# A two-layer trunk on one core: blocks 0 and 1 of the last output product as a pair of seven products

## The chip, the cores and the metric

The kernel runs on one core of one Trainium2 chip. Its engines are TensorE (PE, with the weight loads shown as PEld), VectorE (DVE), ScalarE (ACT), GpSimd (POOL) and SyncE (SP, which here only issues transfers). The metric is the device time of one execution in microseconds; lower is better. Three runs of the kernel before took 1144.73, 1144.99 and 1146.62 us.

## The reference

A residual stream of 256 tokens by 2048 (fp32) goes through two layers, each behind an RMSNorm, and through a last RMSNorm.

```python
def gmlp_branch(xn, w_in, v_g, w_s, b_s, w_out):          # layer 0
    proj = xn @ w_in                                       # [u | v | gate], 3 x 4096
    ...
    y = u * mixed * jax.nn.silu(zg)
    return y @ w_out

def stick_breaking_branch(xn, w_in, w_out):                # layer 1
    proj = xn @ w_in                                       # [q | k | v | gate], 4 x 2048
    q, k, v, zg = jnp.split(proj, 4, axis=-1)
    ...
    o = o.reshape(B, S, SB_WIDTH) * jax.nn.silu(zg)
    return o @ w_out                                       # 2048 x 2048

def reference(x, norm_g, a_w_in, a_v_norm_g, a_w_s, a_b_s, a_w_out, b_w_in, b_w_out, final_g):
    h = x
    for i in range(DEPTH):
        hn = rms_norm(h, norm_g[i])
        ...
        h = h + y
    return rms_norm(h, final_g)
```

The edit is in the last product, `o @ w_out` of layer 1, whose 2048 output columns are four blocks of 512 (blocks 0 to 3).

## The kernel before

**Three terms.** Each fp32 operand is split into a high and a low part (`cut`: ScalarE casts the high part, line 114; VectorE subtracts it, line 115). A product of two tiles is three matmuls, high by high, high by low, low by high (`terms`, lines 119 to 121). Tokens are the stationary side (two tiles of 128, t = 0 and 1), weights the moving side (128 x 512).

**A pair.** `Pair` computes two neighbouring column blocks at once. Of the 16 k tiles of the contraction it takes `ks` tiles from each half (4, or 5 with a "fifth" tile), and does this 2 x 2 block product (two token tiles, two halves of k, two columns) with seven products instead of eight, in the Winograd form. The parts of the weights are named by half and column (`b11`, `b12`, `b21`, `b22`; in tile names b00, b01, b10, b11, then a number for two k tiles). Products p1, p2 and p4 take y itself; p5, p6, p7 and p3 take four sums of y, made once per layer by `sums_of` (tile `ys`) and `fifth` (tile `yse`). The weight sums are made by VectorE in place (lines 286 and 314) and by adding transfers that POOL issues (line 294). `head()` issues p1 and p5, `body()` p6, p2, p7, p3 and p4. Five PSUM banks a, b, c, d, e hold the results; banks a and d are column 0, b and c column 1.

The k tiles left over are plain: `column(0)` adds them to the first column at the end of `body`, and `column(1)` is kept as `pending`, whose steps the next pair takes between its own products (`run`). A raw tile for plain k tiles comes from three buffers (`wraw`), a split tile from five (`wspl`).

**The gates.** The last two pairs of `b_w_in` (bg0, bg2) make the gates. When a column is done, `evac_g` applies SiLU (tiles `bsg` in the buffers sg0 and sg1), and two entries of `queue`, `turn`, transpose it (`gT`), multiply it into `yf`, and split the result into `y_hi` and `y_lo`. Entries of `queue` run between products (`tick`).

**The last product, before.** After bg2 the plain tiles of its second column are flushed. Blocks 0 (f0) and 1 (f1) are `product`s: eight double k tiles, two token tiles, three terms. Beside f0 (`beside_f0`) the queue is drained, the residual h is read back (tile h2), and the sums of y are made at its 10th k tile. f1's steps lie between those of the head of the last pair, f2 (blocks 2 and 3, `KS_F` = 5). `finish` adds the residual, and takes squares and gains. f2's column 1 is done one token tile after the other, so that the first can be stored early (`store`).

**Order.** The program is written in this order, and a scheduler places the instructions of each engine by its own estimate of time. From the middle of bg2 on, `chain` keeps SP's loads in the written order; SP's queue is first in, first out, so a load that waits for its buffer holds back all behind it.

Of the kernel before, what the change touches and what calls it, by code (L numbers as in the profile page):

```python
# [8 lines left out]
F32 = mybir.dt.float32  # L9
F32R = mybir.dt.float32r  # L10
# [4 lines left out]
P = 128  # L15
EPS = 1e-6
NEVER = -1e30
CB = 512
# [11 lines left out]
def trunk_kernel(ctx: ExitStack, tc: tile.TileContext, x, xt, gcols, wst, a_w_in, a_v_norm_g,  # L30
# [11 lines left out]
    nc = tc.nc  # L42
    PSUM = bass.MemoryType.PSUM
    NT, D = x.shape[1], x.shape[2]
# [4 lines left out]
    H = D // P  # L49
# [12 lines left out]
    jk = ctx.enter_context(tc.tile_pool(name="jk", bufs=2))  # L62
# [25 lines left out]
    def f(ap):  # L88
        return ap.bitcast(F32)
# [16 lines left out]
    low = [None]  # L106

    def cut(raw, n, name, by=2):

        hi = wspl.tile([P, 2, CB], F32R, tag="hi", name=f"{name}_hi")  # L110
        lo = wspl.tile([P, 2, CB], F32R, tag="lo", name=f"{name}_lo")
        for i in range(0, n, by):
            sl = slice(i, min(i + by, n))
            nc.scalar.copy(hi[:, sl], raw[:, sl])  # L114
            low[0] = nc.vector.tensor_sub(lo[:, sl], raw[:, sl], f(hi[:, sl]))  # L115
        return hi, lo

    def terms(acc, lh, ll, hi, lo, first, last):
        nc.tensor.matmul(acc, lh, hi, start=first, stop=False, skip_group_check=True)  # L119
        nc.tensor.matmul(acc, lh, lo, start=False, stop=False, skip_group_check=True)  # L120
        nc.tensor.matmul(acc, ll, hi, start=False, stop=last, skip_group_check=True)  # L121
# [78 lines left out]
    queue, wait = [], [0]  # L200

    def tick(n):

        wait[0] -= n
        if wait[0] <= 0 and queue:
            wait[0], work = queue.pop(0)
            work()

    def drain():
        while queue:  # L210
            queue.pop(0)[1]()
# [4 lines left out]
    def ins_of(x):  # L216
        return x.ins if hasattr(x, "ins") else x
# [3 lines left out]
    def load(out, in_, behind=False):  # L221

        ins = ins_of(nc.sync.dma_start(out, in_))
        if behind and not chain:

            tc.add_manual_dep(ins, before[0], NOSYNC, reason="order of loads")
        before[0] = ins.name
        if chain:
            if chain[0] is not None:
                tc.add_manual_dep(ins, chain[0], NOSYNC, reason="order of loads")  # L230
            chain[0] = ins.name
# [139 lines left out]
    adds, pending, prior, ex = [], [], [], None  # L371

    def run(pair):

        tail = pending.pop() if pending else iter(())

        steps = (3 if len(pair.groups) > 2 else 2) * len(pair.groups)
        n, i = prior.pop() if prior else 0, 0

        def between():  # L380
            nonlocal i
            for _ in range((i + 1) * n // steps - i * n // steps if i < steps else 0):
                next(tail, None)
            i += 1
            if i == steps:
                flush(tail)
        for _ in pair.head():
            between()
        pair.body(between)
        pending.append(pair.column(1))  # L390
        prior.append(len(pair.rest) // 2)

    def flush(tail=None):
        for _ in tail if tail is not None else (pending.pop() if pending else ()):
            pass

    def product(src, left, ks, name, evac, before=None):

        banks = [ps_acc.tile([P, CB], F32, tag="acc", name=f"{name}_acc{t}") for t in range(NT)]
        for k0 in ks[::2]:
            if before is not None:
                before(k0)
            raw = wraw.tile([P, 2, CB], F32, tag="raw", name=f"{name}_{k0}_raw")
            load(raw, src(k0, 2))
            hi, lo = cut(raw, 2, f"{name}_{k0}")
            for kk in range(2):
                for t in range(NT):
                    lh, ll = left.part(k0 + kk, t)  # L410
                    terms(banks[t], lh, ll, hi[:, kk, :], lo[:, kk, :], k0 + kk == ks[0], k0 + kk == ks[-1])
            if k0 == ks[-2]:
                for t in range(NT):
                    evac(t, banks[t])
            tick(2)
            yield

    def columns(w, c0, c1):

        w3 = w.rearrange("(k p) n -> p k n", p=P)  # L420

        def src(k0, n, j):
            n0 = (c0, c1)[j]
            return w3[:, k0:k0 + n, n0:n0 + CB]
        return src

    def block_of(w, n0, n):
        w3 = w.rearrange("(k p) n -> p k n", p=P)
        return lambda k0, m: w3[:, k0:k0 + m, n0:n0 + n]
# [7 lines left out]
    def home(tag, shape, dtype, name):  # L437
        return big.tile(shape, dtype, tag=tag, name=name)
# [148 lines left out]
    with ExitStack() as lg:  # L587
# [35 lines left out]
        def evac_gu(b, j, t, bank):  # L623
            y = v_of(t, b * CB, CB)
            sg = jk.tile([P, CB], F32, tag=f"sg{t}", bufs=1, name=f"{'gu'[j]}{b}_{t}")
            nc.scalar.activation(sg, bank, (AF.Silu, AF.Gelu_apprx_tanh)[j], scale=r1[:, t:t + 1])
            if j == 0:
                nc.vector.tensor_mul(y, y, sg)
            else:

                queue.append((1, lambda: times(y, sg)))
# [14 lines left out]
        for b in range(NV):  # L646
            run(Pair(columns(a_w_in, 2 * W + b * CB, b * CB), left, KD, f"gu{b}", KS_GU[b],
                     lambda j, t, bank, b=b: evac_gu(b, j, t, bank), mid=lambda pair, b=b: mid_gu(b, pair), fifth_first=True))
# [147 lines left out]
    p = o_pair(0, None, evac_pair0)  # L796
# [11 lines left out]
    p = o_pair(2, evac_o, mid_o2)  # L808
    p.body(beside(p, g, 1))
    tail = p.column(1)  # L810
    while len(queue) > TPB // 2:
        queue.pop(0)[1]()
    p = Pair(columns(b_w_in, 0, D), left1, KD, "qk0", 4, lambda j, t, bank: evac_qk(0, j, t, bank),
             mid=lambda pair: drain())
# [12 lines left out]
    yf = home("x_hi", [P, H, S], F32, "yf")  # L827
# [171 lines left out]
    pe = y_hi = y_lo = None  # L999
# [9 lines left out]
    def evac_g(hg, t, bank):  # L1009
        sg = gates[t] = jk.tile([P, CB], F32, tag=f"sg{t}", bufs=1, name=f"bsg{hg}_{t}")  # L1010
        nc.scalar.activation(sg, bank, AF.Silu, scale=r2[:, t:t + 1])
        if t == 0:
            return
        sgs = dict(gates)

        def turn(k2):
            pt = ps_ms.tile([P, 2, S], F32, tag="ms", name=f"gT{hg}_{k2}")
            transposed(pt, lambda j, t: sgs[t][:, (k2 * 2 + j) * P:(k2 * 2 + j + 1) * P])
            e0 = hg * TPB + k2 * 2
            sl = slice(e0, e0 + 2)  # L1020
            nc.vector.tensor_mul(yf[:, sl, :], pt, yf[:, sl, :])
            nc.scalar.copy(y_hi[:, sl, :], yf[:, sl, :])
            nc.vector.tensor_sub(y_lo[:, sl, :], yf[:, sl, :], f(y_hi[:, sl, :]))
        for k2 in range(TPB // 2):
            queue.append((1, lambda k2=k2: turn(k2)))

    p.body()
    pending.append(p.column(1))
    prior.append(len(p.rest) // 2)
# [5 lines left out]
    yl = Left(None, None)  # L1035
# [4 lines left out]
    for hg in (0, 2):  # L1040
        run(Pair(columns(b_w_in, 3 * D + hg * CB, 3 * D + (hg + 1) * CB), left1, KD, f"bg{hg}", KS_B,
                 lambda j, t, bank, hg=hg: evac_g(hg + j, t, bank), mid=in_order if hg == 2 else None))
    flush()


    h = gf = None
# [5 lines left out]
    def finish(c, t, acc):  # L1052
        nc.vector.tensor_add(part_of(t, c), acc, part_of(t, c))
        if c == 1:
            later.append((c, t))
        else:
            square_f(c, t, part_of(t, c))
            gain_f(c, t)
# [7 lines left out]
        junk = pe.tile([P, CB], BF16, tag="junk", bufs=2, name=f"junkf{c}_{t}")  # L1066
        nc.scalar.activation(junk, hb, AF.Square, accum_out=sqf[:, t, c:c + 1])

    def beside_f0(k0):

        nonlocal h, gf
        if k0 == 0:
            yl.hi, yl.lo = y_hi, y_lo
        elif k0 == 8:
            drain()
            h = home("v0", [P, NT, D], F32, "h2")
            load_h2(0)
            gf = pe.tile([P, D], F32, name="gf")
            with tc.issue_after(ins_of(low[0])):
                nc.gpsimd.dma_start(gf, final_g.rearrange("(o d) -> o d", o=1).to_broadcast([P, D]))  # L1080
        elif k0 == 10:

            yl.sums_of((yf[:, 0:4], yf[:, 4:8]), 4, home("xs", [P, 2, 4, 4, P], F32R, "ys"), "ys_sm")
            yl.fifth(jk.tile([P, 2, 4, 1, P], F32R, tag="more", bufs=1, name="yse"), "yse")

    def load_h2(c):
        load(h[:, :, c * CB:(c + 1) * CB], hs[:, :, c * CB:(c + 1) * CB])
# [36 lines left out]
    def residual(pair, t):  # L1124
# [2 lines left out]

    last = []

    flush(product(block_of(b_w_out, 0, CB), yl, list(range(H)), "f0", lambda t, bank: finish(0, t, bank), beside_f0))  # L1130
    f1 = product(block_of(b_w_out, CB, CB), yl, list(range(H)), "f1", lambda t, bank: finish(1, t, bank),
                 lambda k0: load_h2(1 + k0 // 4) if k0 in (0, 4, 8) else None)
    p = Pair(columns(b_w_out, 2 * CB, 3 * CB), yl, H, "f2", KS_F,
             lambda j, t, bank: finish(2, t, bank), mid=mid_f)
    for _ in range(2):
        next(f1)
    for _ in p.head():
        next(f1)
    flush(f1)
    p.body()  # L1140


    last = [cut(raw, 2, f"fl_{i}") for i, raw in enumerate(last)]
# [48 lines left out]
```

## Time and profile before

| | |
|---|---|
| runs | 1144.73, 1144.99, 1146.62 us (median 1144.99) |
| profiled execution, first to last instruction (span) | 1142.0 us; the page gives no other time for it |
| median of the runs less the span | 3.0 us |
| TensorE busy | 1132.3 us, 99% of the span |
| VectorE busy | 1010.9 us, 89% |
| ScalarE busy | 828.5 us, 73% |
| HBM read | 259.55 MB, 231 GB/s over the span with what is written |
| mean granted TensorE clock | 0.999 |

"Busy" counts the time in which an instruction runs. TensorE's matmuls are pipelined: each is shown as 0.39 us long, and the next one starts before it ends. The chain of work that ended last is followed back from the last instruction; the share of an engine in it says how much of the span that engine set. Row names leave out buffer numbers: f_p_lo is the low part of a tile of some product p of the pairs f0 and f2, f_lo that of a plain tile.

### The profile page before, as it was taken

Reading aid. Unit: us, or ns where it says so; the run is one execution under the profiler, and the core shown is the slowest. Engines: PE = TensorE matmul, PEld = TensorE weight load, DVE = VectorE, ACT = ScalarE, POOL = GpSimd, SP = SyncE. Lnnn points to the kernel's source line nnn. Section 1 sums busy time; section 2 is a strip of 40 time slices with the busy share of each in tenths; the row PEclk is TensorE's granted clock in tenths of the full one; section 3 lists DMA queues with packets and bytes.
Section 4 is the critical chain, followed back from the end, with each engine's and each line's share of the span. In section 5 each row is a group of like instructions: output and inputs, shape, how many; then the busy total and the mean of one; then the engine's idle time right before and its main releaser. Section 6 shows DMA issues by size and latency. Waiting matters only on the chain.

```text
span 1142.0 us, 14838 instructions
## 1 busy us (share of the span) xinstructions
PE 1132.3 (99%) x5168; PEld 937.6 (82%) x5168; DVE 1010.9 (89%) x1111; ACT 828.5 (73%) x1102; POOL 99.8 (9%) x106
## 2 busy tenths in 40 slices
PE   9999999999999999999999999999999999999997
PEld 6788888888888888888888888888888888888886
DVE  7899889988998999978988678989889989897996
ACT  8776777777777778866657456788678887886564
POOL 0100110110110210100010001110100101100000
PEclk9999999999999999999999999999999999999999
DMA  9988788787797797685885868687687776837972
GB/s 335 317 290 270 214 252 270 194 266 241 173 274 249 191 261 240 177 296 142 267 259 166 276 203 282 153 280 211 181 283 200 211 230 174 272 88 241 325 225 92
DMA packets 135659, 264.72 MB, mean 232 GB/s; under 512 B 8992, under 2 KB 9504, under 8 KB 135456
## 3 DMA queue, kind: packets, MB, share of 16 engines
q1 hardware_dynamic: 117472, 227.57, 58.9%
q0 software_dynamic: 16304, 33.04, 16.2%
q10 hardware_dynamic: 1808, 3.17, 0.8%
q8 instruction: 40, 0.66, 0.2%
q14 instruction: 35, 0.29, 0.1%
HBM read 259.55 MB, written 4.19 MB: 231 GB/s over the span
## 4 chain that ended last, share of the span: by engine, by line
PE 93%; DMA 2%; DVE 2%; issue 1%; ACT 1%; SPq 0%; POOLq 0%; POOL 0%; ACTq 0%; DVEq 0%
PE gu_a L119 3%; PE gu_b L119 3%; PE gu_b L121 3%; PE gu_a L121 3%; PE gu_a L120 3%; PE gu_b L120 3%; PE op_acc L119 2%; PE op_acc L120 2%; PE op_acc L121 2%; PE gu_d L119 2%; PE gu_d L121 2%; PE gu_c L121 2%; PE gu_d L120 2%; PE gu_c L119 2%; PE gu_c L120 2%; PE qk_a L121 1%
## 5 line engine op out<-in xcount | busy, mean ns | idle before, releaser
L114 ACT CAST gu_p_hi<-gu_b 128x1024 fp32r<-128x1024 f32 (+1 forms) x126 | 122.9, 1004 | 38.4 <-DVE gu_b L314 16.1
L115 DVE TENSOR_TENSOR gu_p_lo<-gu_b,gu_p_hi 128x1024 fp32r<-128x1024 f32 (+1 forms) x126 | 142.8, 1165 | 1.9 <-ACT gu_p_hi L114 1.2
L115 DVE TENSOR_TENSOR qk_p_lo<-qk_b,qk_p_hi 128x1024 fp32r<-128x1024 f32 (+1 forms) x77 | 80.8, 1073 | 8.9 <-ACT qk_p_hi L114 8.4
L114 ACT CAST qk_p_hi<-qk_b 128x1024 fp32r<-128x1024 f32 (+1 forms) x77 | 70.5, 934 | 19.0 <-DMA qk_b<-in_b_w_in 4.0
L115 DVE TENSOR_TENSOR gu_lo<-gu_raw,gu_hi 128x1024 fp32r<-128x1024 f32 x60 | 72.1, 1218 | 12.5 <-ACT gu_hi L114 12.2
L114 ACT CAST gu_hi<-gu_raw 128x1024 fp32r<-128x1024 f32 x60 | 62.0, 1052 | 21.0 <-DMA gu_raw<-in_a_w_in 11.5
L115 DVE TENSOR_TENSOR v_lo<-v_raw,v_hi 128x1024 fp32r<-128x1024 f32 (+1 forms) x41 | 48.9, 1193 | 15.2 <-ACT v_hi L114 15.2
L114 ACT CAST v_hi<-v_raw 128x1024 fp32r<-128x1024 f32 (+1 forms) x41 | 41.7, 1028 | 27.9 <-DMA v_raw<-in_a_w_in 26.4
L115 DVE TENSOR_TENSOR v_p_lo<-v_b,v_p_hi 128x1024 fp32r<-128x1024 f32 x42 | 50.3, 1220 | 3.3 <-ACT v_p_hi L114 3.1
L114 ACT CAST v_p_hi<-v_b 128x1024 fp32r<-128x1024 f32 x42 | 43.0, 1049 | 9.8 <-PE v_c L121 4.9
L115 DVE TENSOR_TENSOR bg_p_lo<-bg_b,bg_p_hi 128x1024 fp32r<-128x1024 f32 (+1 forms) x42 | 42.5, 1041 | 4.8 <-ACT bg_p_hi L114 4.7
L114 ACT CAST o_p_hi<-o_b 128x1024 fp32r<-128x1024 f32 (+1 forms) x35 | 33.4, 965 | 18.1 <-PE op_acc L121 13.0
L115 DVE TENSOR_TENSOR bv_p_lo<-bv_b,bv_p_hi 128x1024 fp32r<-128x1024 f32 (+1 forms) x42 | 42.5, 1040 | 3.8 <-ACT bv_p_hi L114 3.6
L114 ACT CAST bv_p_hi<-bv_b 128x1024 fp32r<-128x1024 f32 (+1 forms) x42 | 37.4, 908 | 10.0 <-DMA bv_b<-in_b_w_in 3.0
L294 POOL DMA_DIRECT2D gu_b<-in_a_w_in x20 | 23.0, 1155 | 240.2 <-DVE gu_b L286 134.3
L114 ACT CAST bg_p_hi<-bg_b 128x1024 fp32r<-128x1024 f32 (+1 forms) x42 | 37.3, 907 | 8.0 <-PE bg_a L121 2.5
L115 DVE TENSOR_TENSOR o_p_lo<-o_b,o_p_hi 128x1024 fp32r<-128x1024 f32 (+1 forms) x35 | 38.3, 1113 | 5.4 <-ACT o_p_hi L114 5.4
L286 DVE TENSOR_TENSOR gu_b<-gu_b,gu_b 128x1024 f32<-128x1024 f32 (+1 forms) x36 | 41.4, 1169 | 0.1
L114 ACT CAST o_hi<-o_raw 128x1024 fp32r<-128x1024 f32 x22 | 23.0, 1052 | 24.9 <-DMA o_raw<-in_a_w_out 24.8
L115 DVE TENSOR_TENSOR o_lo<-o_raw,o_hi 128x1024 fp32r<-128x1024 f32 x22 | 26.7, 1221 | 15.2 <-ACT o_hi L114 15.0
L114 ACT CAST op_hi<-op_raw 128x1024 fp32r<-128x1024 f32 x24 | 25.1, 1053 | 19.3 <-PE op_acc L121 8.8
L120 PE MATMUL op_acc<-op_lo,yc 128*128 128x512 f32 x96 | 37.8, 393 | 0.0
(798 smaller groups left out, 3797.8 us busy)
## 6 DMA issues: line engine op xcount, KB each, us to landing
gu_b<-in_a_w_in SPq DMA_DIRECT2D x64, 512.0 KB, 4.8
gu_raw<-in_a_w_in SPq DMA_DIRECT2D x60, 512.0 KB, 5.4
v_raw<-in_a_w_in SPq DMA_DIRECT2D x39, 512.0 KB, 5.5
qk_b<-in_b_w_in SPq DMA_DIRECT2D x32, 512.0 KB, 5.3
qk_raw<-in_b_w_in SPq DMA_DIRECT2D x26, 512.0 KB, 5.5
v_b<-in_a_w_in SPq DMA_DIRECT2D x24, 512.0 KB, 5.4
op_raw<-in_a_w_out SPq DMA_DIRECT2D x24, 512.0 KB, 4.9
o_raw<-in_a_w_out SPq DMA_DIRECT2D x22, 512.0 KB, 4.7
```

Of the source, the lines that this page charges most:

```text
L114: nc.scalar.copy(hi[:, sl], raw[:, sl])
L115: low[0] = nc.vector.tensor_sub(lo[:, sl], raw[:, sl], f(hi[:, sl]))
L119: nc.tensor.matmul(acc, lh, hi, start=first, stop=False, skip_group_check=True)
L120: nc.tensor.matmul(acc, lh, lo, start=False, stop=False, skip_group_check=True)
L121: nc.tensor.matmul(acc, ll, hi, start=False, stop=last, skip_group_check=True)
L286: nc.vector.tensor_sub(into[g], b0[g], b1[g])
L294: adds.append(nc.gpsimd.dma_start(into[g], self.src(HALVES[i][k], n, j), accum_op=ALU.add))
```

## The change

Blocks 0 and 1 become a `Pair` with four k tiles from each half (f0, `ks` = 4). It is run like the pairs ahead: its head and body take the steps of bg2's second column between their products, and its own second column lies between the products of f2. The turns of the second gate block are called before it (`turned` notes which are done), the sums of y are made ahead of it, and what stood beside f0 moves to its middle (`mid_f0`, called between p4 and the plain tiles of column 0).

```diff
+            turned.append(e0)
...
-    flush()
...
-        if k0 == 0:
-            yl.hi, yl.lo = y_hi, y_lo
-        elif k0 == 8:
-            drain()
...
-        elif k0 == 10:
-
-            yl.sums_of((yf[:, 0:4], yf[:, 4:8]), 4, home("xs", [P, 2, 4, 4, P], F32R, "ys"), "ys_sm")
-            yl.fifth(jk.tile([P, 2, 4, 1, P], F32R, tag="more", bufs=1, name="yse"), "yse")
+    def mid_f0(pair):
+        drain()
+        h = home("v0", [P, NT, D], F32, "h2")
+        load_h2(0)
+        load_h2(1)
...
+        yl.fifth(jk.tile([P, 2, 4, 1, P], F32R, tag="more", bufs=1, name="yse"), "yse")
...
-    flush(product(block_of(b_w_out, 0, CB), yl, list(range(H)), "f0", lambda t, bank: finish(0, t, bank), beside_f0))
-    f1 = product(block_of(b_w_out, CB, CB), yl, list(range(H)), "f1", lambda t, bank: finish(1, t, bank),
-                 lambda k0: load_h2(1 + k0 // 4) if k0 in (0, 4, 8) else None)
+    while H // 2 - 2 not in turned:
+        queue.pop(0)[1]()
+    yl.hi, yl.lo = y_hi, y_lo
+    yl.sums_of((yf[:, 0:4], yf[:, 4:8]), 4, home("xs", [P, 2, 4, 4, P], F32R, "ys"), "ys_sm")
+    run(Pair(columns(b_w_out, 0, CB), yl, H, "f0", 4, lambda j, t, bank: finish(j, t, bank), mid=mid_f0))
+    load_h2(2)
+    load_h2(3)
...
-    for _ in range(2):
-        next(f1)
-    for _ in p.head():
-        next(f1)
-    flush(f1)
-    p.body()
+    run(p)
+    pending.clear()
```

Three places of the order show it. In the names, f0_p40 is the first two k tiles of f0's product p4, f0_08 the plain double tile of k 8 and 9 in column 0, f0_18 the same in column 1, and ys the sums of y.

VectorE, where the sums of y are made. Before, this is in the second half of block 0 and the start of block 1:

```order
L1023 TENSOR_TENSOR y_lo_9017<-yf_6081,y_hi_9016 128x512
L115 TENSOR_TENSOR f0_12_lo_9581<-f0_12_raw_9578,f0_12_hi_9580 128x1024
L184 TENSOR_TENSOR ys_9532<-ys_sm_0_9533,ys_9532 128x512
L1023 TENSOR_TENSOR y_lo_9017<-yf_6081,y_hi_9016 128x512
L184 TENSOR_TENSOR ys_9532<-ys_sm_1_9534,ys_9532 128x512
L115 TENSOR_TENSOR f0_14_lo_9599<-f0_14_raw_9596,f0_14_hi_9598 128x1024
L189 TENSOR_TENSOR ys_sm_0_9533<-yf_6081 128x512
L190 TENSOR_TENSOR ys_sm_1_9534<-yf_6081,ys_sm_1_9534 128x512
L115 TENSOR_TENSOR f1_0_lo_9628<-f1_0_raw_9625,f1_0_hi_9627 128x1024
L184 TENSOR_TENSOR ys_9532<-ys_sm_0_9533,ys_9532 128x512
```

VectorE, the same sums now, between the products of f0:

```order
L286 TENSOR_TENSOR f0_b00_1_9371<-f0_b10_1_9503,f0_b00_1_9371 128x1024
L115 TENSOR_TENSOR f0_p21_lo_9552<-f0_b10_1_9503,f0_p21_hi_9551 128x1024
L115 TENSOR_TENSOR f0_p70_lo_9563<-f0_b01_0_9373,f0_p70_hi_9562 128x1024
L190 TENSOR_TENSOR ys_sm_1_9356<-yf_6081,ys_sm_1_9356 128x512
L184 TENSOR_TENSOR ys_9354<-ys_sm_0_9355,ys_9354 128x512
L115 TENSOR_TENSOR f0_p71_lo_9573<-f0_b01_1_9375,f0_p71_hi_9572 128x1024
L115 TENSOR_TENSOR f0_p30_lo_9587<-f0_b11_0_9424,f0_p30_hi_9586 128x1024
L334 TENSOR_TENSOR f0_b_9507<-f0_b_9507,f0_es_9509 128x512
L115 TENSOR_TENSOR f0_p31_lo_9597<-f0_b11_1_9426,f0_p31_hi_9596 128x1024
L115 TENSOR_TENSOR f0_p40_lo_9607<-f0_b00_0_9369,f0_p40_hi_9606 128x1024
L184 TENSOR_TENSOR ys_9354<-ys_sm_1_9356,ys_9354 128x512
```

Per plain tile two or three operations on sums stood ahead; now they lie among tiles of seven products that themselves need differences of weights, and the fourth sum stands behind p4's first tile.

VectorE, the eviction of block 0 (line 1053 before, 1054 now). Before:

```order
L286 TENSOR_TENSOR f2_b00_0_9661<-f2_b01_0_9667,f2_b00_0_9661 128x1024
L168 TENSOR_TENSOR yse_sm_9549<-yse_full_9548,yse_sm_9549 128x128
L170 TENSOR_TENSOR yse_sm_9549<-yse_full_9548,yse_sm_9549 128x128
L1053 TENSOR_TENSOR h2_9510<-f0_acc0_9428,h2_9510 128x512
L1053 TENSOR_TENSOR h2_9510<-f0_acc1_9429,h2_9510 128x512
L172 TENSOR_TENSOR yse_9547<-yse_sm_9549,yse_9547 128x512
L1063 TENSOR_TENSOR h2_9510<-h2_9510,gf_9512 128x512
L115 TENSOR_TENSOR f1_4_lo_9688<-f1_4_raw_9685,f1_4_hi_9687 128x1024
```

The same eviction on VectorE now, at the head of f2:

```order
L115 TENSOR_TENSOR f2_p12_lo_9761<-f2_b00_2_9731,f2_p12_hi_9760 128x512
L286 TENSOR_TENSOR f2_b00_0_9727<-f2_b01_0_9733,f2_b00_0_9727 128x1024
L1054 TENSOR_TENSOR h2_9627<-f0_a_9377,h2_9627 128x512
L286 TENSOR_TENSOR f2_b00_1_9729<-f2_b01_1_9735,f2_b00_1_9729 128x1024
L1054 TENSOR_TENSOR h2_9627<-f0_d_9582,h2_9627 128x512
L286 TENSOR_TENSOR f2_b00_2_9731<-f2_b01_2_9737,f2_b00_2_9731 128x512
L1064 TENSOR_TENSOR h2_9627<-h2_9627,gf_9630 128x512
L115 TENSOR_TENSOR f0_18_lo_9770<-f0_18_raw_9767,f0_18_hi_9769 128x1024
L115 TENSOR_TENSOR f2_p50_lo_9797<-f2_b00_0_9727,f2_p50_hi_9796 128x1024
```

The eviction, which reads f0's finished banks, stands between differences of f2's weights and ahead of f0_18, the first plain tile of block 1.

SP's loads around the last plain tile of block 0 (14 before, 014 now). Before:

```order
L223 DMA f0_14_raw_9596<-in_b_w_out 128x2x512
L223 DMA h2_9510<-hs_4513 128x2x512
L223 DMA f1_0_raw_9625<-in_b_w_out 128x2x512
L223 DMA f1_2_raw_9643<-in_b_w_out 128x2x512
L223 DMA f2_b00_0_9661<-in_b_w_out 128x2x512
L223 DMA f2_b00_1_9663<-in_b_w_out 128x2x512
L223 DMA f2_b00_2_9665<-in_b_w_out 128x512
```

SP's loads there now:

```order
L223 DMA f0_014_raw_9699<-in_b_w_out 128x2x512
L223 DMA h2_9627<-hs_4513 128x2x512 x2
L223 DMA f2_b00_0_9727<-in_b_w_out 128x2x512
L223 DMA f2_b00_1_9729<-in_b_w_out 128x2x512
L223 DMA f2_b00_2_9731<-in_b_w_out 128x512
L223 DMA f2_b01_0_9733<-in_b_w_out 128x2x512
L223 DMA f2_b01_1_9735<-in_b_w_out 128x2x512
L223 DMA f2_b01_2_9737<-in_b_w_out 128x512
L223 DMA f0_18_raw_9767<-in_b_w_out 128x2x512
```

The first loads of f2 follow the last plain tile of block 0 without plain tiles between them, and the first plain tile of block 1 stands behind them.

More of the change, by code (lines that the diff above doesn't have):

```diff
@@ L1023, in turn @@
             nc.vector.tensor_sub(y_lo[:, sl, :], yf[:, sl, :], f(y_hi[:, sl, :]))
+            turned.append(e0)
         for k2 in range(TPB // 2):
             queue.append((1, lambda k2=k2: turn(k2)))
+    turned = []
     p.body()
@@ L1067, in square_f @@
         nc.scalar.activation(junk, hb, AF.Square, accum_out=sqf[:, t, c:c + 1])
-    def beside_f0(k0):
+    def mid_f0(pair):
         nonlocal h, gf
-        if k0 == 0:
-            yl.hi, yl.lo = y_hi, y_lo
-        elif k0 == 8:
-            drain()
[L1076 to L1080, printed above, removed]
-        elif k0 == 10:
-            yl.sums_of((yf[:, 0:4], yf[:, 4:8]), 4, home("xs", [P, 2, 4, 4, P], F32R, "ys"), "ys_sm")
-            yl.fifth(jk.tile([P, 2, 4, 1, P], F32R, tag="more", bufs=1, name="yse"), "yse")
+        drain()
+        h = home("v0", [P, NT, D], F32, "h2")
+        load_h2(0)
+        load_h2(1)
+        gf = pe.tile([P, D], F32, name="gf")
+        with tc.issue_after(ins_of(low[0])):
+            nc.gpsimd.dma_start(gf, final_g.rearrange("(o d) -> o d", o=1).to_broadcast([P, D]))
+        yl.fifth(jk.tile([P, 2, 4, 1, P], F32R, tag="more", bufs=1, name="yse"), "yse")
     def load_h2(c):
```

## The prediction

> **What bounds the kernel now.** I read the chain that ended last, then what TensorE waits for, then the busy time by stretch around the edit, then VectorE's timeline there, since it writes the low half of each weight tile that TensorE multiplies.
>
> ```profile
> span 1142.0 us, 14838 instructions
> PE 93%; DMA 2%; DVE 2%; issue 1%; ACT 1%; SPq 0%; POOLq 0%; POOL 0%; ACTq 0%; DVEq 0%
> PE wps L79 <- DVE warm L76: 1.3, 1, 1.3
> PE v_acc L120 <- DVE v_lo L115: 0.6, 1, 0.6
> PE gT L434 <- ACT bsg L1011: 0.2, 1, 0.2
> ...
> 982.00:1026.90 44.90, 44.90 (x220) 37.86 (x219) 40.72 (x45) 38.83 (x51) 4.17 (x4) 1.00 0.53 140
> 1026.90:1060.00 33.10, 32.91 (x161) 27.13 (x160) 24.85 (x30) 22.07 (x30) 0.56 (x1) 1.00 0.73 236
> 1060.00:1102.90 42.90, 42.90 (x191) 35.53 (x190) 38.09 (x48) 23.48 (x31) 4.14 (x4) 1.00 0.91 296
> 1102.90:1126.00 23.10, 23.10 (x104) 19.04 (x103) 22.77 (x27) 16.44 (x22) 0.00 (x0) 1.00 0.36 115
> ```
>
> TensorE holds the chain, and once started it waits under 1 us in all. So a matmul removed is time gained, as long as TensorE goes on finding its operands ready. Columns of the last four rows: stretch, length, then busy time of PE, weight load, DVE, ACT, POOL, then granted clock, DMA share, GB/s. From 1026.9 to 1102.9 (the last gate pair's plain k tiles, blocks 0 and 1, the first products of the last pair) VectorE is busy 24.85 + 38.09 = 62.9 of 76.0 us: 13.1 us are free. Behind that it is full: 22.77 of 23.10.
>
> **Removed: twelve matmuls.** Blocks 0 and 1 took 2 x 16 k tiles x 2 token tiles x 3 terms = 192 products of 128x512. The pair takes 7 x 4 x 3 = 84, and 8 k tiles x 2 columns x 2 x 3 = 96: 180.
>
> ```profile
> 1130.52 0.39 PE L119 MATMUL f_c<-fl_hi,y_hi 128*128 128x512 f32 x1
> 1134.37 0.39 PE L121 MATMUL f_c<-fl_hi,y_lo 128*128 128x512 f32 x1
> 1034.27 0.65 PE gT L434 x6
> ```
>
> These are the first and last of 18 in a row: (1134.37 - 1130.52) / 17 = 0.2265 us each; a transpose is 0.65 / 6 = 0.11. Term one: 12 x 0.2265 = **-2.7 us**.
>
> **Added: VectorE work.** The pair cuts 7 x 2 + 4 + 4 = 22 double tiles where 16 were cut, and forms 6 sums or differences of double tiles: 12 more operations of 128x1024. Two sums with a bank copy make two more of 128x512. The sums of y, the turns of the gates and the evictions keep their number and only move.
>
> ```profile
> 1057.65 0.68 DVE L185 TENSOR_TENSOR ys_sm<-yf 128x512 f32<-128x512 f32 x1
> 1058.25 0.68 DVE L1021 TENSOR_TENSOR yf<-gT,yf 128x512 f32<-128x512 f32 x1
> 1068.81 0.89 DVE L165 TENSOR_TENSOR yse_full<-y_hi,y_lo 128x128 f32<-128x128 f32 x4
> 1069.62 0.28 DVE L169 TENSOR_TENSOR yse_sm<-yse_full 128x128 f32<-128x128 f32 x1
> 1116.98 3.48 DVE L115 TENSOR_TENSOR f_lo<-f_raw,f_hi 128x1024 fp32r<-128x1024 f32 x3
> 1120.38 3.48 DVE L115 TENSOR_TENSOR fl_lo<-fl_raw,fl_hi 128x1024 fp32r<-128x1024 f32 x3
> ```
>
> Back to back, start to start: 3.40 / 3 = 1.135 us for 128x1024, 0.60 for 128x512, 0.81 / 4 = 0.20 for 128x128. The addition is 12 x 1.135 + 2 x 0.60 = 14.8 us, and it must be done in 2.7 us less. The 13.1 free microseconds are short of that by 14.8 + 2.7 - 13.1 = 4.4 us, unless VectorE has a lead to spend. So I keep two accounts from a point that both kernels share.
>
> ```profile
> 1026.97 1.22 DVE L115 TENSOR_TENSOR bg_lo<-bg_raw,bg_hi 128x1024 fp32r<-128x1024 f32 x1
> 1027.98 0.40 PE L119 MATMUL bg_a<-bg_hi,x 128*128 128x512 f32 x1
> 1029.12 0.69 DVE L1023 TENSOR_TENSOR y_lo<-yf,y_hi 128x512 fp32r<-128x512 f32 x1 [0.33 <-ACT y_hi L1022]
> 1031.58 1.23 DVE L115 TENSOR_TENSOR bg_lo<-bg_raw,bg_hi 128x1024 fp32r<-128x1024 f32 x1 [1.15 <-ACT bg_hi L114]
> ```
>
> VectorE starts the low part of the last gate pair's tile 010 at 1026.97, TensorE its first product at 1027.98: there is no lead. The next two idles, 0.33 + 1.15 = 1.48 us, lie before the two orders part and stay.
>
> - To the low part of f0's product p4 (f0_p40) VectorE has 25 operations of 128x1024 and 20 of 128x512 ahead and with it: 28.4 + 12.0, so 1067.4, and 1068.9 with the 1.48. TensorE has 151 products and 18 transposes before it needs that tile: 34.2 + 2.0, so 1064.1. TensorE is then late by 4.8 us (by the same count it is 3.0 at p71, three tiles earlier).
> - The eviction of block 0 (h2<-f0_a) now stands in VectorE's order between two differences of f2's tiles. TensorE reaches the end of f0_a after 219 products and 24 transposes, at 1080.2, with the delay 1085.0, and the last product takes 0.39 more. VectorE arrives at 1084.4 and waits 1.0 us; in the kernel before the like wait was 0.5:
>
> ```profile
> 1126.18 0.69 DVE L1053 TENSOR_TENSOR h<-f_a,h 128x512 f32<-128x512 f32 x1 [0.52 <-PE f_a L121]
> ```
>
> - To the low part of block 1's first plain tile (f0_18) VectorE has 35 of 128x1024, 32 of 128x512, 8 of 128x128: 39.7 + 19.3 + 1.6 = 60.6, so 1087.6. TensorE needs it after 237 products and 24 transposes: 53.7 + 2.6, so 1084.3. The gap is 3.3; with 1.48 and 1.0 it is **+5.8 us**, term two. Later tiles up to the last (f2_014) need no more by the same accounts (f0_114 and f2_p71 come within 0.4 us of it).
>
> Term three is what VectorE idles beside that, which no row of before can show, since there it never led the time here.
>
> ```profile
> 1000.00:1010.00 10.00, 10.00 (x56) 8.65 (x55) 9.38 (x11) 8.60 (x13) 0.86 (x1) 1.00 0.40 76
> 1010.00:1020.00 10.00, 10.00 (x47) 8.35 (x46) 9.65 (x12) 8.38 (x11) 0.00 (x0) 1.00 0.36 105
> ```
>
> Low end 0: from 1096.56 to 1126.18 it runs without a gap. High end: in these windows it idles 0.97 of 20 us, 5%, over the 56 us from 1034 to 1090 that is 2.7. Nearest is the stretch without a gap, where VectorE was needed, but it had fewer short links to ScalarE; I take **+0.9**. A gain in this term is excluded: the account already packs the operations.
>
> Sum: -2.7 + 5.8 + 0.9 = +4.0 us: a span of 1146.0 for this execution's 1142.0. The median of the runs shown, 1144.99, lies 3.0 above the span, and becomes **1149.0**.
>
> **Costed at nothing, with the cover.** ScalarE: six more casts of 1.05 us and four bank copies of 0.6, some 8.7 us; it sat idle for transfers far longer:
>
> ```profile
> L114 ACT CAST f_hi<-f_raw 128x1024 fp32r<-128x1024 f32 x16 | 16.8, 1049 | 16.3 <-DMA f_raw<-in_b_w_out 14.9 <-PE f_acc L121 1.3
> f_b<-in_b_w_out POOLq DMA_DIRECT2D x2, 512.0 KB, 9.3
> SPq L223 <- DVE f_lo L115: 29.7, 14, 3.7
> ```
>
> POOL's queue gets two adding transfers of 512 KB; a like one landed 9.3 us after issue, and they are issued behind f0's first differences (about 1039) and first read by p7's casts (about 1058). The last gates' SiLU now waits until VectorE has read the sums of y that share its tiles (sg0, sg1), to about 1064.0 and 1069.8; behind it on ScalarE is the copy into f0_d that p4 needs, ready about 1068, before p4's low part at 1068.9. If VectorE were quicker, that copy would be next. The sums of y also come earlier on TensorE's path: their first low part is due at 1053 and made at 1054, inside the 4.8. SP's queue is past in the rivals. The last 18 products and the stores are untouched.
>
> **Rivals.**
> *Faster: VectorE keeps up.* Layer 0's pairs have the same seven products by four, and TensorE never waits there; then only term one counts: 1142.3. For it: VectorE was busy 40.72 of 44.90 in the pair before, so a pair's own work fits. Against: here the sums and turns of y, two evictions and a pair of five follow closely. It decides where the 60.6 us to f0_18 become 55, with 1.03 us for each 128x1024 and the rest in proportion; no row is that short.
> *The transfers become the bound.* SP takes its loads in order, and f0's last plain tile (014) must wait until VectorE has read 08 (three raw buffers), to about 1072.4. Behind it stand two h blocks, six tiles of f2 and f0_18:
>
> ```profile
> 1070.00:1080.00 10.00, 10.00 (x46) 8.29 (x45) 8.52 (x13) 5.43 (x9) 1.20 (x1) 1.00 1.07 353
> 1090.00:1100.00 10.00, 10.00 (x46) 8.28 (x45) 9.57 (x10) 5.78 (x8) 0.85 (x1) 1.00 0.88 268
> ```
>
> 4.7 MB at 353 GB/s take 13.4 us and end at 1085.8, cast and low part at 1088: in time for 1090.1. At 268 GB/s it is 17.6 us, 1092.2, and 2.1 us more: 1151.1.
> *The clock falls.* TensorE's waits could come in one piece and its clock drop. The slow pace is seen at the start:
>
> ```profile
> 1.29 4.02 PE L79 MATMUL wps<-warm 128*128 128x512 bf16 x9 [1.29 <-DVE warm L76]
> 1130.00:1142.00 12.00, 4.76 (x22) 3.60 (x20) 2.72 (x6) 4.05 (x8) 1.12 (x2) 0.91 0.47 175
> ```
>
> Nine products in 4.02 us are 0.45 each, twice 0.2265; one relapse of the same length costs 9 x 0.22 = 2.0 us: 1151.0. In the accounts no single wait is over 1.8 us (p4's), and the granted clock fell only in the last window, where TensorE idles for over 7 us. The Trainium skill (TensorE: Matmul & The Clock Gate, Why this matters for your kernels) says to leave no idle gap over about 3 us between bursts, or the clock goes back to half. By that rule too the waits here are too short to cost anything, and only a single stall twice as long as accounted would; the fall to 0.91 agrees with it.
>
> **How the numbers follow.** VectorE late by terms two and three, 1147.3 to 1150.5: 0.68. Transfers as well: 0.12, 1150.5 to 1153. Clock: 0.03. VectorE late, but by no more than half as much, 1143.5 to 1147.3: 0.10. Hidden, 1142.3: 0.07. A measurement of this kernel tells 0.2%, 2.3 us, from no change. Slower 0.81 (the first three and a little less), same 0.11, faster 0.08. The range, 1146.0 to 1152.0, takes the first case, most of the second and the edge of the fourth; its ends are near terms one and two without the 1.0 and 1.48 (+0.6), and the sum with 2.7 for term three and with the late transfers (+7.9).
>
> **What would show it.** TensorE 12 matmuls fewer, and waits for f0's and f2's low parts by VectorE in its list, 5 to 8 us together, most at p2 to p4 and at f0_18; VectorE above 9.7 of 10 from 1035 to 1125; products unchanged at 0.2265; the clock at 1.00 up to the last pair's end. I am wrong if TensorE waits less than 3 us there, if its waits end with ScalarE casts behind transfers, or if VectorE's 128x1024 come closer than 1.135.

## The result, and the profile after

The changed kernel takes **1158.01 us** (1157.52 to 1163.46, four runs) against 1145.76 of the kernel before, measured beside it: 12.25 us more, ratio 1.0116, 95% interval 1.0091 to 1.0141. The forecast was 1149.0 with a range of 1146.0 to 1152.0. The direction was right; the loss is three times as large.

First the page, then the list of TensorE's waits from 1030 us on (engine, what it waited for, us in total, times, longest).

```profile
span 1156.2 us, 14847 instructions
PE 85%; DMA 6%; DVE 4%; issue 2%; ACT 1%; POOL 1%; SPq 1%; POOLq 0%; ACTq 0%; DVEq 0%
PE f_b L119 <- ACT f_hi L114: 3.7, 2, 2.6
PE f_a L120 <- DVE f_p_lo L115: 0.9, 1, 0.9
PE f_b L120 <- DVE f_lo L115: 0.9, 1, 0.9
PE f_a L119 <- ACT f_p_hi L114: 0.7, 1, 0.7
```

TensorE had 93% of the chain and has 85%; DMA went from 2% to 6%. The two longest waits, 3.7 us together, end with a ScalarE cast of a plain tile (f_hi), not with VectorE's low parts: what the prediction named as the sign that it is wrong. Now the stretch around the edit in pieces of 10 us. Columns: PE, weight load, DVE, ACT, POOL, granted clock, DMA share, GB/s.

```profile
1050.00:1060.00 10.00, 9.27 (x41) 7.27 (x39) 10.00 (x14) 7.11 (x10) 0.00 (x0) 1.00 1.04 317
1060.00:1070.00 10.00, 8.70 (x38) 6.37 (x36) 10.00 (x13) 8.87 (x12) 0.00 (x0) 1.00 0.01 2
1070.00:1080.00 10.00, 9.21 (x42) 7.11 (x43) 10.00 (x15) 4.35 (x6) 0.00 (x0) 1.00 0.32 103
1080.00:1090.00 10.00, 10.00 (x46) 8.29 (x45) 7.28 (x12) 4.83 (x7) 0.00 (x0) 1.00 1.03 361
1090.00:1100.00 10.00, 7.85 (x26) 5.50 (x25) 10.00 (x12) 6.77 (x11) 3.32 (x3) 0.83 1.07 334
1100.00:1110.00 10.00, 7.39 (x31) 5.71 (x30) 5.63 (x7) 3.59 (x6) 0.85 (x1) 0.94 0.92 229
```

From 1050 to 1080 VectorE is full (10.00) and TensorE waits for it, as forecast. But from 1060 to 1070 the DMA engines stand still (share 0.01, 2 GB/s), and later VectorE idles: 7.28 of 10, then 5.63. The transfers start too late and then hold back the engine that sets the pace. SP's timeline tells why (start, time it took to issue, count):

```profile
1045.02 30.95 SPq L223 DMA_DIRECT2D f_raw<-in_b_w_out  x4
1076.03 1.19 SPq L223 DMA_DIRECT2D h<-hs  x2
1077.26 3.69 SPq L223 DMA_DIRECT2D f_b<-in_b_w_out  x6
1081.27 0.37 SPq L223 DMA_DIRECT2D f_raw<-in_b_w_out  x1
1089.51 6.16 SPq L223 DMA_DIRECT2D f_raw<-in_b_w_out  x2
```

The four loads of f0's plain tiles take SP 30.95 us, because the last, 014, waits for the raw buffer of 08, which VectorE reads at 1074.37. Only then come h2, six tiles of f2, f0_18 and, at 1089.51, f0_112. ScalarE's timeline has three casts that wait for loads, and VectorE's three low parts that wait for these casts; the row at 1094.06 is f0_18, ahead of which VectorE does not idle (in brackets the idle time ahead, and what ended it):

```profile
1079.70 1.05 ACT L114 CAST f_hi<-f_raw 128x1024 fp32r<-128x1024 f32 x1 [3.89 <-DMA f_raw<-in_b_w_out]
1084.81 1.05 ACT L114 CAST f_p_hi<-f_b 128x1024 fp32r<-128x1024 f32 x1 [3.03 <-DMA f_b<-in_b_w_out]
1106.58 1.04 ACT L114 CAST f_hi<-f_raw 128x1024 fp32r<-128x1024 f32 x1 [6.07 <-DMA f_raw<-in_b_w_out]
1080.78 1.23 DVE L115 TENSOR_TENSOR f_lo<-f_raw,f_hi 128x1024 fp32r<-128x1024 f32 x1 [0.72 <-ACT f_hi L114]
1085.90 1.23 DVE L115 TENSOR_TENSOR f_p_lo<-f_b,f_p_hi 128x1024 fp32r<-128x1024 f32 x1 [1.96 <-ACT f_p_hi L114]
1094.06 1.21 DVE L115 TENSOR_TENSOR f_lo<-f_raw,f_hi 128x1024 fp32r<-128x1024 f32 x1
1107.66 1.23 DVE L115 TENSOR_TENSOR f_lo<-f_raw,f_hi 128x1024 fp32r<-128x1024 f32 x1 [4.37 <-ACT f_hi L114]
```

The waits are for 014, the first tile of f2 (p10) and f0_112. The chain of work that ended last runs through the same places (start, us; four of its pieces):

```profile
1074.45 1.14 DVE f_lo L115
1079.89 9.55 DMA f_b<-in_b_w_out
1089.51 16.97 DMA f_raw<-in_b_w_out
1106.58 1.05 ACT f_hi L114
```

VectorE reads 08 (its low part), the held transfers start, one of f2's tiles lands after 9.55 us, and the load of f0_112, issued then, takes another 16.97. And TensorE, twice: the first product of f0_112, and the clock in pieces of 2 us behind it and behind f0_18.

```profile
1107.68 0.50 PE L119 MATMUL f_b<-f_hi,y_hi 128*128 128x512 f32 x1 [2.61 <-ACT f_hi L114]
1096.00:1098.00 2.00, 2.00 (x6) 1.57 (x5) 2.00 (x3) 1.57 (x2) 0.00 (x0) 0.50 1.11 262
1110.00:1112.00 2.00, 2.00 (x6) 1.59 (x5) 2.00 (x3) 1.94 (x3) 0.00 (x0) 0.50 0.38 126
```

The granted clock is 0.50 in both; VectorE (third value) is full in both.

**A ledger for comparing kernels.** What lies ahead of the edit varies by some us from profile to profile (after reaches the mark below 2.98 us later than before, 1.7 of it one wait of TensorE in layer 0), so I measure from a mark that all share, VectorE's low part of bg2's tile 010, to its last low part (fl_lo). Over that stretch VectorE's busy time (the third value) and its idle time add up to the length:

```profile
1026.97:1123.86 96.89, 96.70 (x442) 79.88 (x441) 83.82 (x101) 61.92 (x82) 4.70 (x5) 1.00 0.74 239
```
```profile
1029.95:1137.35 107.40, 99.62 (x429) 79.06 (x428) 97.85 (x115) 70.63 (x92) 7.12 (x7) 0.97 0.69 223
```

The first is before, the second after. VectorE's work grew by 97.85 - 83.82 = 14.0 us; 14.8 was forecast. Its idle time went only from 13.07 to 9.55 us, so the stretch grew by 10.5 us. That is what the two profiles put at the edit, for 12.25 by the medians. The question for the experiments: why can't VectorE use these 9.55 us?

### The profile page after: what moved, and what is told of

Its sections match the earlier page's. It is cut to its first block, busy times and chain, and to the rows that moved or that the text cites. A ratio compares the mean times of both kernels' runs of the same rounds, so it can differ in the third digit from the quotient of the medians.

```text
span 1156.2 us, 14847 instructions
## 1 busy us (share of the span) xinstructions
PE 1136.0 (98%) x5156; PEld 936.8 (81%) x5156; DVE 1024.9 (89%) x1125; ACT 837.7 (72%) x1112; POOL 106.8 (9%) x108
## 4 chain that ended last, share of the span: by engine, by line
PE 85%; DMA 6%; DVE 4%; issue 2%; ACT 1%; POOL 1%; SPq 1%; POOLq 0%; ACTq 0%; DVEq 0%
PE gu_a L121 2%; PE gu_b L121 2%; PE gu_a L120 2%; PE gu_b L120 2%; PE gu_a L119 2%; PE gu_b L119 2%; PE op_acc L121 2%; PE op_acc L120 2%; PE op_acc L119 2%; PE gu_d L119 2%; DMA v_raw<-in_a_w_in 2%; PE gu_d L121 2%; PE gu_d L120 2%; PE gu_c L120 2%; PE gu_c L121 2%; PE gu_c L119 2%
## 5 line engine op out<-in xcount | busy, mean ns | idle before, releaser
L114 ACT CAST gu_hi<-gu_raw 128x1024 fp32r<-128x1024 f32 x60 | 61.9, 1051 | 19.9 <-DMA gu_raw<-in_a_w_in 10.5
L115 DVE TENSOR_TENSOR v_lo<-v_raw,v_hi 128x1024 fp32r<-128x1024 f32 (+1 forms) x41 | 48.8, 1193 | 14.9 <-ACT v_hi L114 14.8
L114 ACT CAST bg_p_hi<-bg_b 128x1024 fp32r<-128x1024 f32 (+1 forms) x42 | 37.2, 907 | 8.0 <-PE bg_a L121 2.5
L114 ACT CAST f_p_hi<-f_b 128x1024 fp32r<-128x1024 f32 (+1 forms) x35 | 33.1, 963 | 13.6 <-PE f_c L121 5.6
L115 DVE TENSOR_TENSOR f_p_lo<-f_b,f_p_hi 128x1024 fp32r<-128x1024 f32 (+1 forms) x35 | 37.9, 1110 | 2.7 <-ACT f_p_hi L114 2.7
L114 ACT CAST op_hi<-op_raw 128x1024 fp32r<-128x1024 f32 x24 | 25.1, 1053 | 19.4 <-DMA op_raw<-in_a_w_out 9.5
L115 DVE TENSOR_TENSOR qk_lo<-qk_raw,qk_hi 128x1024 fp32r<-128x1024 f32 x26 | 31.4, 1219 | 8.4 <-ACT qk_hi L114 8.4
```

## The experiments

T is the theory that the held queue of loads (014's buffer) makes the loss beyond the forecast, V that VectorE's added work does, C that the clock does. All times are medians, each with its own interval against runs of the kernel before on the same chip.

| kernel | us | against before (95%) | us over before | VectorE busy, idle |
|---|---|---|---|---|
| after | 1158.01 | 1.0091 to 1.0141 | 12.3 | 97.85, 9.55 |
| 014 in a buffer of its own | 1148.96 | 1.0019 to 1.0046 | 4.1 | 97.12, 3.51 |
| after, no weight sums of f0 | 1158.91 | 1.0081 to 1.0159 | 14.1 | 91.13, 16.47 |
| after, extra products | 1159.38 | 1.0095 to 1.0145 | 14.5 | 97.94, 13.27 |
| pair with two k tiles | 1150.36 | 1.0032 to 1.0068 | 5.5 | 91.35, 9.56 |
| own buffer, four sums fewer | 1145.66 | 0.9982 to 1.0005 | 0.1 | 92.86, 4.01 |
| pair with two k tiles, own buffers | 1146.78 | 0.9996 to 1.0023 | 1.3 | 91.35, 6.59 |
| own buffer, sums on POOL | 1151.31 | 1.0027 to 1.0056 | 5.8 | 98.94, 3.61 |
| after, plain transfers for adding ones | 1152.99 | 1.0037 to 1.008 | 7.5 | 97.60, 6.93 |
| the same with extra products | 1152.68 | 1.0037 to 1.0076 | 7.3 | 97.58, 7.38 |

**An own buffer for 014.** f0's last plain raw tile of column 0 takes a buffer of the pair that is free after product p2, so that it no longer waits for VectorE to read 08.

```diff
-raw = wraw.tile([P, 2, CB], F32, tag="raw", ...)
+own = self.name == "f0" and j == 0 and ks[0] == 14
+raw = (sraw if own else wraw).tile([P, 2, CB], F32, tag="b21_0" if own else "raw", ...)
```

> Only change against the changed kernel: f0's last plain tile of column 0 (014) has a raw buffer of its own (b21_0, free after f0's p2), so that SP need not hold h2, f2's tiles and block 1's plain tiles until VectorE has read 08. Theory T (transfers held behind 014 add to VectorE's lateness, and the clock falls in the waits): f2's first load is issued about 1072 instead of 1077, plain tiles 18 and 112 arrive 4 to 5 us earlier, TensorE's waits behind f0_18 and f0_112 shrink from 5.2 to about 2 us, one or both half-clock stretches go: 1150 to 1153 against 1158. Rival V (only VectorE's work sets it, the transfers just follow): within 1 us of 1158.

It gave 1148.96 us, just under what T had named, and 8 us less than after (12.3 - 4.1). SP's timeline and the ledger of this kernel, VectorE's one long wait with the cast behind it, and two products of TensorE:

```profile
1042.76 16.53 SPq L223 DMA_DIRECT2D f_raw<-in_b_w_out  x4
```
```profile
1027.69:1128.32 100.63, 96.19 (x430) 77.15 (x429) 97.12 (x115) 70.74 (x92) 7.08 (x7) 1.00 0.74 238
```
```profile
1102.33 0.69 DVE L115 TENSOR_TENSOR f_p_lo<-f_b,f_p_hi 128x512 fp32r<-128x512 f32 x1 [2.02 <-ACT f_p_hi L114]
1101.68 0.62 ACT L114 CAST f_p_hi<-f_b 128x512 fp32r<-128x512 f32 x1 [3.26 <-DMA f_b<-in_b_w_out]
1069.90 0.50 PE L120 MATMUL f_d<-f_p_lo,y_hi 128*128 128x512 f32 x1 [0.39 <-DVE f_p_lo L115]
1103.78 0.50 PE L119 MATMUL f_b<-f_hi,y_hi 128*128 128x512 f32 x1 [0.95 <-ACT f_hi L114]
```

The four loads take 16.53 us instead of 30.95, VectorE's idle time falls from 9.55 to 3.51, its work stays nearly the same (97.12 for 97.85), and the granted clock is 1.00. In after, 0.72 + 1.96 + 4.37 = 7.05 us of the idle time stand behind loads; here it is 2.02. So T holds: the stretch is 6.8 us shorter. One thing moved besides the loads: the scheduler placed VectorE and TensorE anew from 014 on, and f0_18's low part now stands ahead of block 0's eviction. This kernel does not separate the two; the one with plain transfers below, whose order is that of after, does in part.

**VectorE's sums left out, the queue held as in after.**

```diff
 def minus(...):
+    if self.name == "f0": continue
...
     for g in range(len(self.b22)):
+        if self.name == "f0": continue
         nc.vector.tensor_add(self.b11[g], self.b22[g], self.b11[g])
```

> Leaves out VectorE's six sums and differences of f0's weights (6 x 1.135 = 6.8 us; the products then read other numbers). V: TensorE is not late any more at p4 (5.0 us in the changed kernel), and nothing else is wrong: near 1146. T: the lateness at p4 goes, and 014 is issued some 6 us earlier, but the transfers behind it still take about 30 us to f0_112, so TensorE still waits 3 to 5 us there and loses one half-clock stretch (1.7): 1149 to 1152.

Six operations fewer, and no gain: 1158.91 us. Both theories missed it. The two adding transfers, which no longer waited for a difference, left 4 to 6 us earlier and met the loads of bg2's plain tiles. From this kernel, ScalarE's wait for such a tile and VectorE's behind it, and SP's loads:

```profile
1047.90 1.04 ACT L114 CAST bg_hi<-bg_raw 128x1024 fp32r<-128x1024 f32 x1 [5.57 <-DMA bg_raw<-in_b_w_in]
1048.98 1.23 DVE L115 TENSOR_TENSOR bg_lo<-bg_raw,bg_hi 128x1024 fp32r<-128x1024 f32 x1 [6.29 <-ACT bg_hi L114]
```
```profile
1044.65 31.12 SPq L223 DMA_DIRECT2D f_raw<-in_b_w_out  x4
```

What VectorE saved, 6.7 us, it lost again in one wait of 6.29 us, and 014 was held as long as in after (31.12 us). VectorE's idle time rose to 16.47. So this kernel doesn't tell V from T: it moved a second set of transfers into the way.

**The same question on the good queue.** On top of the own buffer, four of the six sums are left out, the two ahead of p6 and the two ahead of p4; no transfer waits for these.

> The kernel in which f0's last plain raw tile 014 has a buffer of its own (1148.96 us, transfers out of the way, clock full), and four of f0's six weight sums on VectorE left out (the two ahead of p6, the two ahead of p4; neither starts a transfer). Theory V (what is left of the loss is VectorE's work): 4 x 1.135 = 4.5 us less ahead of p4 and of f0_18, TensorE's 5 us lateness at p4 shrinks to about 1 and the time to 1143.5 to 1145.5. Rival S (what is left are links with ScalarE, bank copies or the shape of the pair): 1147.5 to 1150.

1145.66 us: 3.3 less than with the sums, and not told from before (0.9982 to 1.0005). Its ledger:

```profile
1027.65:1124.52 96.87, 94.43 (x429) 77.13 (x428) 92.86 (x111) 70.16 (x92) 7.12 (x7) 1.00 0.77 247
```

97.12 - 92.86 = 4.3 us less work, and the stretch is 3.8 us shorter; TensorE has no wait over 0.1 us any more up to 1098. V is shown for what is left once the loads come in time, though it gave a little less than the 4.5 us that it promised, and the time is 0.2 us above the range that it named.

**Extra products for TensorE.** Nine products into an unused bank ahead of f0_18 and eleven ahead of f0_112 fill TensorE's pauses, so that its clock should stay up.

```diff
+if self.name == "f0" and j == 1 and ks[0] in (8, 12):
+    fill(9 if ks[0] == 8 else 11)      # ordered behind the product ahead
```

> Adds 9 products into an unused bank before f0_18's first product and 11 before f0_112's, about as long as the waits there (2.2 and 2.6 us). Theory C (waits of under 3 us each lead to a half-clock stretch of 3.4 us, 1.7 us lost each time): no half-clock stretch, 20 more products, and 2 to 3.4 us less than the changed kernel: 1154.5 to 1156. If the clock falls for another reason: the same stretches, 1158, or later by what the filling overshoots.

1159.38 us, no gain. The first pause shrank to 0.87 us and the clock stayed at 1.00 there, but TensorE then waited 3.54 us instead of 2.61 for f0_112, and the clock fell there instead. C missed at the first pause; the second was not closed, so there it stays untested.

**Adding transfers made plain.** f2's four transfers that add in flight move the same bytes to the same tiles without adding (f2's sums are left out); the order of every engine stays word for word.

```diff
-adds.append(nc.gpsimd.dma_start(into[g], src, accum_op=ALU.add))
+adds.append(nc.gpsimd.dma_start(into[g], src, **({} if self.name == "f2" else {"accum_op": ALU.add})))
```

> The changed kernel with f2's adding transfers (the weight sums that POOL issues, 1.5 MB) as plain transfers of the same bytes to the same tiles, so these sums are left out; the order of every engine is the same. Theory A (adding transfers hold up the others): the rate in the 10 us after they are issued stays above 330 GB/s instead of 262, f0_112's load lands earlier, and the 2.6 us wait there with the 1.7 us at half clock behind it go or halve: 1153.5 to 1155.5 us. Theory B (the bytes alone do it): the rate falls to about 262 GB/s all the same, and the time stays at 1157 to 1159.

1152.99 us, a little better than theory A had named. From the queues of after and of this kernel, both between 1085 and 1110 us (packets, MB, share of the 16 engines' time), and one piece of this kernel, to be read beside that of 262 GB/s shown above:

```profile
q0 software_dynamic: 832, 1.57, 34.0%
```
```profile
q0 software_dynamic: 448, 1.57, 17.0%
1096.00:1098.00 2.00, 2.00 (x7) 1.56 (x6) 2.00 (x3) 0.95 (x1) 0.00 (x0) 0.59 1.03 382
```

The same 1.57 MB take 34.0% of the engines' time when they add and 17.0% when they don't, and with the engines full the rate is 262 against 382 GB/s. The wait ahead of f0_112 is gone. How much of the loss that is depends on the measure: 12.3 - 7.5 = 4.8 us by the medians, whose intervals reach 2.5 to 3 us to each side, and 107.40 - 104.53 = 2.9 us by the ledger. The own buffer saved 8.2 and 6.8 us by the same two measures. So 3 to 5 us of what it saved come from adding transfers that stand in the way of late loads, and the rest, 3 to 4 us, goes with the late start itself and the changed order.

**The clock, alone.** In the last kernel TensorE waits 1.73 us ahead of f0_18, then 0.22 and 0.57 us, and the clock is halved. It is down at 1090.86, ahead of the 0.57:

```profile
1090.02 0.50 PE L119 MATMUL f_b<-f_hi,y_hi 128*128 128x512 f32 x1 [1.73 <-ACT f_hi L114]
1090.86:1092.00 1.14, 0.80 (x1) 0.29 (x1) 1.14 (x2) 1.14 (x3) 0.55 (x1) 0.50 1.07 395
```

Eight extra products fill the 1.73.

> The kernel with f2's transfers as plain ones (sums left out; 1152.99 us), and eight extra products of 128x512 into a bank that is not used, ahead of TensorE's first product of f0_18, so that the 1.73 us wait there is filled and only 0.22 + 0.57 stay. Nothing else moves. Theory C (the short waits in a row halve the clock): the granted clock stays 1.00 behind that place (0.50 from 1092 to 1096 without the extra products), 12 products at 0.43 us come at 0.2265, and the time falls by 2 to 3 us, to 1150 to 1151. Rival (the clock falls for another reason, or VectorE sets the pace there anyway): 1152.5 to 1153.5 us.

1152.68 us: no difference that can be told from 1152.99. One piece of it, to compare with 0.59 in the piece above, and TensorE's wait next in line:

```profile
1096.00:1098.00 2.00, 1.94 (x8) 1.61 (x9) 2.00 (x3) 2.00 (x5) 0.00 (x0) 1.00 1.04 390
1104.89 0.50 PE L119 MATMUL f_b<-f_hi,y_hi 128*128 128x512 f32 x1 [0.58 <-ACT f_hi L114]
```

The extra products did hold the clock at 1.00, and the time stayed. VectorE is full there with or without them; TensorE at full pace comes earlier to the next tile and waits (0.58 us; without the extra products it has no wait there). The ledgers agree: the stretches are 104.96 and 104.53 us, and the kernel with extra products was already 0.9 us later at p4, ahead of them (first product with its low part 43.1 us after the mark, for 42.2). That leaves some 0.4 us for the half clock, where C promised 2 to 3. So it was mostly a symptom here; the 3.4 us that C put down to it in after (two stretches of 1.7) are not confirmed.

**Half the pair.** f0 with two k tiles from each half, once with the shared raw buffers, once with own buffers for 012 and 014.

```diff
-run(Pair(columns(b_w_out, 0, CB), yl, H, "f0", 4, ...))
+run(Pair(columns(b_w_out, 0, CB), yl, H, "f0", 2, ...))
...
+own = {12: "b22_1", 14: "b21_1"}.get(ks[0]) if self.name == "f0" and j == 0 else None   # second kernel
```

> f0 as a pair with two k tiles from each half instead of four: 6 products fewer than before (1.4 us), VectorE with 6 operations of 128x1024 and two of 128x512 more (8.0 us, within the 13.1 free). V: TensorE is never late, 1143 to 1145 (before is 1145.8). T: SP is still held by 014, now behind six plain tiles of column 0, and the transfers of f2 come late against a TensorE that is not late: some 2 to 4 us of waits and one half-clock stretch, 1147 to 1151.

> The pair f0 with two k tiles from each half (1150.36 us with shared buffers), and its last two plain raw tiles of column 0 (012 and 014) in buffers of their own. It adds 6 operations of 128x1024 and 2 of 128x512 on VectorE, 8.0 us, which fit the 13.1 free ones, and removes 6 matmuls, 1.4 us. Theory T (shared raw buffers delayed its loads): 1144 to 1146.5, near the kernel before. Rival (casts, or the places where VectorE's work falls): 1148 to 1151.

1150.36 and 1146.78 us. The own buffers are worth 3 to 4 us here too, in the same way: VectorE's work is the same, 91.35 us, and its idle time 9.56 and 6.59 us. The second missed its 1144 to 1146.5 by 0.3 and is not told from the kernel before; six matmuls (1.4 us) are not to be seen in it.

**The sums on POOL.** On top of the own buffer, VectorE's sums ahead of p6 are made by POOL. The expectation says four; the edit's test missed the two ahead of p4, which stayed on VectorE.

> As the kernel with the own buffer for 014 (1148.96 us), but four of f0's weight sums (the two ahead of p6, the two ahead of p4) are computed by POOL instead of VectorE; nothing is left out. Theory V: VectorE has 4.5 us less, POOL's time is hidden behind the products between, 1144 to 1146. Rival P (POOL is slow: its one wide operation in the trace, 128x256, takes 1.1 us, by elements 4.4 us for 128x1024; or the two engines slow each other): p6's tiles come late, TensorE waits 3 to 8 us there, 1150 to 1156.

1151.31 us; the interval reaches into that of the own buffer alone (1.0019 to 1.0046), so no gain, and more likely a loss. POOL's two sums, VectorE's two operations beside them, and TensorE's wait:

```profile
1045.02 7.77 POOL L314 TENSOR_TENSOR f_b<-f_b,f_b 128x1024 f32<-128x1024 f32 x2 [1.47 <-DVE f_p_lo L115]
1047.71 2.83 DVE L115 TENSOR_TENSOR bg_lo<-bg_raw,bg_hi 128x1024 fp32r<-128x1024 f32 x1
1050.46 2.88 DVE L185 TENSOR_TENSOR ys_sm<-yf 128x512 f32<-128x512 f32 x1
1056.93 0.50 PE L121 MATMUL f_e<-f_p_hi,ys 128*128 128x512 f32 x1 [2.15 <-DVE ys L184]
```

VectorE was relieved of 2 x 1.135 = 2.3 us and lost (2.83 - 1.22) + (2.88 - 0.68) = 3.8 us while POOL worked. TensorE waited 2.15 us for a sum of y, not for p6's tiles as the rival said.

## Why the prediction was right and where it failed

**Term one, -2.7 us.** Twelve matmuls fewer (5156 for 5168), 0.2265 us apart as before. Nothing in the runs shows it as a gain, since TensorE waits for VectorE and the loads here; it stands in the sum as time in which VectorE has less room.

**Terms two and three, +6.7 us: the account was right, its agreement with one kernel in part luck.** To p4's first low part the account said 1068.9, and this profile's mark is 2.98 later: 1071.9. VectorE ended it at 1072.11. TensorE's first product with it came 5.0 us later than its own count said; 4.8 was forecast. To the end of f0_18's low part 65.3 us passed from the mark (1094.06 + 1.21 - 1029.95). The account's 60.6 + 1.48, with the 0.72 and 1.96 us that VectorE waited behind loads, makes 64.8, so some 0.5 us is left for term three (+0.9). The wait of 1.0 us for block 0's banks did not come.

The kernel with the own buffer lost 4.1 us (interval 0.19% to 0.46%, 2.2 to 5.3 us) where the sum was +4.0. It too is 5.0 us late at p4 (1069.90 - 1027.69 = 42.2 us after the mark, where TensorE's count of 151 products and 18 transposes gives 37.2). But behind that it doesn't wait at f0_18, where the account had one more microsecond, and does wait 0.95 us for a cast that stands behind a late load. That both come to 4 us is in part luck. Leaving out four of the sums gave most of it back.

**The failed step: the cover of the transfers, "in time for 1090.1".** The sum has no term for transfers. The rival that they become the bound had the mechanism and the place, even SP's release (1072.4; with the mark's shift 1075.4, measured 1076.03), but it was given 0.12 and 2.1 us, where the own buffer shows 7 to 8 us. It tested one tile of the queue, f0_18, against its need, and that tile was in time: VectorE did not idle ahead of it. But each tile of the queue has its own need. 014 and p10, which stand ahead of f0_18, were needed at once; their casts waited 3.89 and 3.03 us, and VectorE 0.72 and 1.96. And f0_112, behind it, was left to the sentence that later tiles need no more "by the same accounts", which count VectorE's work and take every cast as ready; its load took 16.97 us, and it came 4.37 us late for VectorE.

**The rate.** 353 and 268 GB/s were taken as two ends of one unknown. They are closer to two conditions: plain transfers ran at 382 to 390 with the engines full, and adding ones, which POOL issues right among the late loads, brought it to 262. In the kernel before, the row with 268 had a share of only 0.88; the prediction didn't ask what else was on the engines.

**The clock.** The prediction said that only a single wait twice as long as accounted would halve it, and leaned on the Trainium skill (TensorE: Matmul & The Clock Gate, Why this matters for your kernels), which sets the mark at gaps over about 3 us. The traces disagree on the size: single waits of 1.73 us (plain transfers), 1.99 (no weight sums), 2.15 (sums on POOL) and 2.61 (after) were followed by 3.4 us or more at 0.50, and so were 1.06 + 0.22 + 0.87 within 3.4 us (after). Single waits of 1.56 (own buffer, four sums fewer), 1.57 (two k tiles) and 1.61 us (sums on POOL) were not. But with VectorE full beside it, it moved little that the runs can tell.

**The other rivals.** VectorE keeps up: refuted by the 5.0 us at p4, and by the kernel with the own buffer, whose stretch holds 97.12 us of its work and 3.51 idle. That the loss lies below half of the account came true only with four sums left out.

## What to carry to other kernels

A first-in, first-out queue of loads is as late as the engine that frees its buffers: when a change makes that engine the bound, follow every load behind the waiting one to the moment its own reader needs it, not only the last one, and ask which other transfers run then. A buffer of its own for the one load that blocks was worth 7 to 8 us, more than leaving out four of the sums (3.3). Still, no kernel here beat the one before; the best that leaves nothing out, two k tiles with own buffers, is not told from it. And before relieving TensorE of 2.7 us at the price of 14 on an engine that has 13 free, see that these can be used: idle time behind late data can't be.

## What the runs showed of the hardware

- Adding transfers took twice the DMA engines' time of plain ones of the same bytes (34.0% against 17.0% for 1.57 MB).
- A wait of 1.73 us on TensorE, behind a long run without gaps, was followed by half clock (products 0.43 us apart instead of 0.2265); a wait of 1.61 us was not.
- A POOL sum of 128x1024 took 3.9 us beside a busy VectorE, and two VectorE operations took 2.83 and 2.88 us beside it instead of 1.22 and 0.68. That agrees with the Trainium skill (SBUF — State Buffer, Who interferes with whom), by which a VectorE instruction with two inputs in SBUF contends with a GpSimd instruction that reads SBUF.
